# Splitting q and k once in the projection and storing them in three token orders, in a hybrid RWKV-7 and dilated-attention layer

## The chip, the cores and the metric

The kernel runs on one core of a Trainium2 chip, in one launch. The metric is device time in microseconds, the median of three runs. Engines are named as in the profile: PE (matmuls; PEld are its weight loads), DVE, ACT, POOL, and SP, whose queue starts most of the DMAs.

## The reference

One decoder layer over 2048 tokens of width 1024: a projection, two mixers side by side (an RWKV-7 recurrence on 512 columns, dilated attention with 8 heads of 64 on the other 512), an output projection, and a SwiGLU feed-forward of width 2816. What the change touches is the attention's three branches, which see the same q, k and v in three token orders:

```python
DILATED_PAIRS = ((128, 1), (512, 4), (2048, 16))
...
def to_sub(t):
    t = t.reshape(B, H, L, dilation, Dh).transpose(0, 1, 3, 2, 4)
...
s = jnp.einsum('bhrnqe,bhrnke->bhrnqk', qb, kc) * (Dh ** -0.5)
...
pe = jnp.exp(s - m)
den = jnp.sum(pe, axis=-1, keepdims=True)
o = jnp.einsum('bhrnqk,bhrnke->bhrnqe', pe, vc) / den
```

With dilation r, a token t belongs to the subsequence t mod r, and a query block of 128 of that subsequence sees its own and the previous block. The three results are mixed by a softmax over their log-sums.

## The kernel before

**Products in parts.** A float32 operand is written as a high part (rounded to the PE's fast format, `F32R`) plus a low part (the rest). A dense product is three matmuls of 128x512 (`three`, L220 to L223). Weights come through the class `Weights`: a DMA on SP's queue (L197), a cast on ACT for the high part (L207), a subtraction on DVE for the low part (L209), with 2 raw and 3 split buffers.

**Projection (0 to about 900 us).** `dense_in` takes four blocks of 512 tokens. For each it runs 26 column tiles `ct` of 128 columns; tiles 14 to 17 are q and 18 to 21 are k, two heads in each. Such a tile is copied from PSUM by ACT (L489) and written to the DRAM tensors `qT` or `kT` by one DMA on ACT's queue (L493). The RWKV recurrence runs beside it: a generator `drive` takes dense steps between its steps, and this fixes PE's order by hand. The other engines' orders are made by the scheduler. Tiles of the pool `sp` are shared by tag ("kx", "kkh", "Pd", "mshift" belong to the recurrence and to the token shift).

**Attention.** `heads_b` runs five parts: `attention(0)` (branches 1 and 2 of block 0, and block 0 of branch 3), `branch3` (all of dilation 16), `attention(1)`, `(2)` and `(3)`. Each goes over 8 heads and cuts a head into `Unit`s, 32 in each part. A unit computes scores on PE (L950, L951: q's high half against k's high and low part), mask and row minimum on DVE (L955), exponentials on ACT (L960), transposes on PE (L967) with a copy on ACT or DVE by turns (L971), and values (L981). Dense products of the output projection, and later of the feed-forward, are put between, again by `drive`, with a fixed cost `ATT` for each attention step.

Before a head's units its q and k are loaded and split. `load_dup` (L928 to L930) loads 64 rows twice, into both halves of the 128 partitions, from SP's queue. `split_q` (L921, L922) and `split_k` (L925, L926) then cast on ACT and subtract on DVE, once for the plain token order and once more through a strided view for dilation 4; `branch3` does the same with stride 16, four pieces of 512 tokens for q and for k of each head:

```python
q2 = qq[:, TB:].rearrange("p (r i) -> p r i", r=4)
...
split_q(q2, rq.rearrange("p (i r) -> p r i", r=4))
split_k(kh2, kl2, rk_all[:, TB - back :].rearrange("p (n i r) -> p r n i", r=4, i=P))
```

The split of head h+1 (`prep`) runs beside head h where a second set of buffers is free (`spare`, `q2nd`), else between the heads.

Of the kernel before, what the change touches and what calls it, by code (L numbers as in the profile page):

```python
# [37 lines left out]
BR = ((128, 1), (512, 4), (2048, 16))  # L38
NEG = -1.0e30
# [7 lines left out]
def tile_hybrid_layer(  # L47
# [41 lines left out]
    qT = dram.tile([W, S], F32, name="qT")  # L89
    kT = dram.tile([W, S], F32, name="kT")  # L90
# [140 lines left out]
    F_COST = 3.0, 1.0, 1.0, 0.0, 0.0  # L231
# [40 lines left out]
    def constants():  # L272
# [6 lines left out]
        for hi, low, src, tag, lo, zero in (  # L279
            (w2d, w2lo, decay_w2[0], "L", slice(0, HD), slice(HD, P)),  # L280
            (a2d, a2lo, iclr_a2[0], "kkh", slice(HD, P), slice(0, HD)),
        ):
            nc.gpsimd.memset(f32(low[zero]), 0.0)
            raw = sp.tile([P, W], F32, name="wa_raw", tag=tag)
# [84 lines left out]
    def dense_in():  # L369
# [58 lines left out]
        for b in range(nblocks):  # L428
            t0 = b * TB
            for at, ct in enumerate(ORDER):  # L430
# [26 lines left out]
                if ct < SHIFT_TILES:  # L457
# [28 lines left out]
                    got[b, ct] = o  # L486
                else:
                    o = sp.tile([P, TB], F32, name="qkv", bufs=1)
                    nc.scalar.copy(out=o, in_=pd)  # L489
                    if ct < 22:  # L490
                        dst = qT if ct < 18 else kT
                        r0 = ((ct - 14) % 4) * P
                        nc.scalar.dma_start(out=dst[r0 : r0 + P, t0 : t0 + TB], in_=o)  # L493
                    else:

                        def turn_v(o=o, ct=ct, t0=t0):
                            pt = ps_t.tile([P, NT, P], F32, name="pv", tag="t")
                            for i in range(NT):
                                nc.tensor.transpose(pt[:, i, :], o[:, i * P : (i + 1) * P], ident)
                            o2 = sp.tile([P, NT, 2, HD + 1], F32, name="vn", tag="mshift", bufs=1)  # L500
                            nc.gpsimd.memset(o2[:, :, :, HD : HD + 1], 1.0)
                            nc.scalar.copy(out=o2[:, :, :, 0:HD], in_=pt.rearrange("p i (h d) -> p i h d", d=HD))
                            h0 = (ct - 22) * 2
                            nc.scalar.dma_start(
                                out=vN[t0 : t0 + TB, h0 : h0 + 2, :].rearrange("(i p) h d -> p i (h d)", p=P),
                                in_=o2.rearrange("p i h d -> p i (h d)"),
                            )

                        later.append(turn_v)
                done.add((b, ct))  # L510

    def rwkv():
# [3 lines left out]
        for b in range(nblocks):  # L516
# [8 lines left out]
            def start_pair(j):  # L525
# [33 lines left out]
                Pd = sp.tile([P, NCH, CH + 1], F32, name="Pd")  # L559
# [40 lines left out]
            for j in range(NPAIR):  # L600
# [8 lines left out]
                kkh = sp.tile([P, TB], F32, name="kkh")  # L609
# [293 lines left out]
    R3 = BR[2][1]  # L903
# [15 lines left out]
    def split_q(hi, raw):  # L919

        nc.scalar.copy(out=hi, in_=raw)  # L921
        nc.vector.tensor_tensor(out=hi[HD:P], in0=raw[HD:P], in1=f32(hi[HD:P]), op=ALU.subtract)  # L922

    def split_k(hi, lo, raw):
        nc.scalar.copy(out=hi, in_=raw)  # L925
        nc.vector.tensor_tensor(out=lo, in0=raw, in1=f32(hi), op=ALU.subtract)  # L926

    def load_dup(dst, src):  # L928
        nc.sync.dma_start(out=dst[0:HD], in_=src)
        nc.sync.dma_start(out=dst[HD:P], in_=src)  # L930
# [5 lines left out]
    class Unit:  # L936
# [7 lines left out]
        def scores(self):  # L944
# [4 lines left out]
            for g, (q, kh, kl) in enumerate(self.group):  # L949
                nc.tensor.matmul(ps[:, g, :], lhsT=q, rhs=kh, start=True, stop=False)  # L950
                nc.tensor.matmul(ps[:, g, :], lhsT=q, rhs=kl, start=False, stop=True)  # L951
# [97 lines left out]
    NK = R3 * P  # L1049
    q_all = ap.tile([P, NK], F32R, name="q_all")  # L1050
    k_all = ap.tile([P, 2, NK], F32R, name="k_all")
    rk_all = ap.tile([P, 2 * TB], F32, name="rk_all")
    sides, spare = [], []

    def heads_of(head, prep, second, after):


        for h in range(HEADS):
            nxt = None
            if h + 1 < HEADS:  # L1060
                second[h + 1] = h % 2 == 0 and bool(spare)
                nxt = prep(h + 1)
            elif after:
                nxt = after()
                next(nxt)
            beside = second[h] or h + 1 < HEADS and second[h + 1]
            if nxt and beside:
                sides.insert(0, nxt)
            yield from head(h)
            if nxt and beside:  # L1070
                if nxt in sides:
                    sides.remove(nxt)
                for _ in nxt:
                    pass
            elif nxt:
                yield lambda nxt=nxt: nxt

    def attention(b):
# [4 lines left out]
        n1, n2 = TB + lead, TB + back  # L1083
        vs, raws, cur, second = {}, {}, {}, {0: False}
# [8 lines left out]
        def load_v(hp):  # L1093
# [10 lines left out]
            vs[hp] = v1, v2  # L1104

        def load_qk(h):
            hs = slice(h * HD, (h + 1) * HD)
            rq = ap.tile([P, TB], F32, name="rq", tag="rq", bufs=2)
            load_dup(rq, qT[hs, t0 : t0 + TB])
            load_dup(rk_all[:, TB - back :], kT[hs, t0 - back : t0 + TB])  # L1110
            raws[h] = rq

        def prep(h):
            rq = raws.pop(h)
            if second[h]:
                kh, kl = spare[0][:, 0, 0 : n1 + n2], spare[0][:, 1, 0 : n1 + n2]
            else:
                kh, kl = k_all[:, 0, 0 : n1 + n2], k_all[:, 1, 0 : n1 + n2]
            if second[h] and not b:

                qq = spare[0].rearrange("p a n -> p (a n)")[:, n1 + n2 : n1 + n2 + 2 * TB]
            else:
                qq = q_all[:, (h % 2) * 2 * TB : (h % 2 + 1) * 2 * TB]

            q1, kh1, kl1 = qq[:, 0:TB], kh[:, 0:n1], kl[:, 0:n1]
            split_q(q1, rq)
            split_k(kh1, kl1, rk_all[:, TB - lead :])
            yield 0.0

            q2 = qq[:, TB:].rearrange("p (r i) -> p r i", r=4)  # L1130
            kh2 = kh[:, n1:].rearrange("p (r n i) -> p r n i", r=4, n=nb)
            kl2 = kl[:, n1:].rearrange("p (r n i) -> p r n i", r=4, n=nb)
            split_q(q2, rq.rearrange("p (i r) -> p r i", r=4))
            split_k(kh2, kl2, rk_all[:, TB - back :].rearrange("p (n i r) -> p r n i", r=4, i=P))
            cur[h] = q1, kh1, kl1, q2, kh2, kl2
            if h + 1 < HEADS:
                load_qk(h + 1)
            yield 0.0
            yield False
            if h % 2 and h + 1 < HEADS:  # L1140
                load_v((h + 1) // 2)
            yield False

        def head(h):
            q1, kh1, kl1, q2, kh2, kl2 = cur.pop(h)
            v1, v2 = vs[h // 2]
            hl = h % 2
            for m0, m1 in ((0, 1), (1, 3), (3, 4)) if b == 0 else ((0, 2), (2, 4)):
# [542 lines left out]
```

## Time and profile before

| | us |
|---|---|
| runs, median (lowest to highest) | 3007.9 (3002.45 to 3013.22) |
| the profiled execution | 3003.22 |
| its span, first to last instruction | 3001.3 |
| PE busy | 2881.1 (96%) |
| PE weight loads busy | 2381.6 (79%) |
| DVE busy | 1957.3 (65%) |
| ACT busy | 1405.2 (47%) |
| POOL busy | 383.7 (13%) |
| bytes moved | 358.67 MB, mean 120 GB/s |

Busy is the time in which an engine executes; shares are of the whole span and hide that the stages differ. The granted clock is PE's speed as the throttle let it run, 1.00 being 2.4 GHz and 0.50 the lower level of 1.2 GHz. "Landing" is the time from a DMA's start on its queue to the arrival of its last byte.

### The profile page before, as it was taken

How to read it: one execution, taken by the hardware profiler on the slowest of the kernel's cores; microseconds unless marked ns; L12 is line 12 of the kernel's file. 1: busy time of each engine (PE TensorE's matmuls, PEld its weight loads, DVE VectorE, ACT ScalarE, POOL GpSimd, SP SyncE). 2: the span in 40 equal slices, each digit the busy share in tenths (PEclk: the TensorE clock that was granted, in tenths of full speed). 3: DMA queues.
4: the chain of work that ended last, by engine and by line, in shares of the span. 5: the costliest groups of instructions: out<-in, count | busy, mean ns of one | idle time of the engine just before them, and what ended most of it. 6: DMA issues, size and time to landing. Idle time of an engine off the chain costs nothing. (4 is left out here: it accounts for less than half of the span.)

```text
span 3001.3 us, 47441 instructions
## 1 busy us (share of the span) xinstructions
PE 2881.1 (96%) x17457; PEld 2381.6 (79%) x17457; DVE 1957.3 (65%) x3974; ACT 1405.2 (47%) x2688; POOL 383.7 (13%) x543
## 2 busy tenths in 40 slices
PE   8999999998998888899999999999999999999998
PEld 6777777776777777788888888888888888888887
DVE  6877788786868877766665585656675444554444
ACT  5534544544536666655544464434453332342233
POOL 1123113112103221000100010001010100000001
PEclk9999999999998999899999999999999999999999
DMA  4332332332233777454444454444344333333333
GB/s 127 102 100 74 94 104 78 100 105 60 61 100 117 226 230 240 133 140 124 128 146 118 132 157 119 117 125 124 113 138 127 107 101 97 102 120 98 96 98 102
DMA packets 456716, 358.67 MB, mean 120 GB/s; under 512 B 26610, under 2 KB 384548, under 8 KB 456484
## 3 DMA queue, kind: packets, MB, share of 16 engines
q1 hardware_dynamic: 419348, 318.35, 36.6%
q10 hardware_dynamic: 32656, 22.62, 2.5%
q0 software_dynamic: 4480, 14.68, 1.3%
q8 instruction: 137, 2.24, 0.3%
q14 instruction: 95, 0.78, 0.1%
HBM read 311.19 MB, written 44.37 MB: 118 GB/s over the span
## 5 line engine op out<-in xcount | busy, mean ns | idle before, releaser
L209 DVE TENSOR_TENSOR wlo<-wraw,whi 128x512 fp32r<-128x512 f32 x800 | 566.0, 708 | 618.4 <-ACT whi L207 613.3
L207 ACT CAST whi<-wraw 128x512 fp32r<-128x512 f32 x800 | 495.4, 620 | 944.3 <-PE acc L223 257.1
L221 PE MATMUL pd<-h_hi,whi 128*128 128x512 f32 (+1 forms) x840 | 350.6, 417 | 3.4 <-DVE r L466 1.6
L222 PE MATMUL pd<-h_lo,whi 128*128 128x512 f32 (+1 forms) x840 | 329.9, 393 | 1.0 <-DVE h_lo L386 0.8
L223 PE MATMUL pd<-h_hi,wlo 128*128 128x512 f32 (+1 forms) x840 | 329.7, 392 | 0.1
L221 PE MATMUL acc<-whi,a_hi 128*128 128x512 f32 x704 | 286.6, 407 | 0.7 <-DVE x L1505 0.7
L221 PE MATMUL pg<-fh_hi,whi 128*128 128x512 f32 x704 | 284.0, 403 | 1.9 <-ACT whi L207 1.3
L221 PE MATMUL pu<-fh_hi,whi 128*128 128x512 f32 x704 | 284.6, 404 | 0.0
L223 PE MATMUL acc<-whi,a_lo 128*128 128x512 f32 x704 | 276.0, 392 | 0.0
L223 PE MATMUL pu<-fh_hi,wlo 128*128 128x512 f32 x704 | 275.8, 392 | 0.0
L223 PE MATMUL pg<-fh_hi,wlo 128*128 128x512 f32 x704 | 275.8, 392 | 0.0
L222 PE MATMUL pg<-fh_lo,whi 128*128 128x512 f32 x704 | 274.6, 390 | 0.0
L222 PE MATMUL acc<-wlo,a_hi 128*128 128x512 f32 x704 | 274.5, 390 | 0.0
L222 PE MATMUL pu<-fh_lo,whi 128*128 128x512 f32 x704 | 274.4, 390 | 0.0
L960 ACT ACTIVATE pr<-pr,mx 128x256 f32<-128x256 f32 (+1 forms) x416 | 162.7, 450 | 104.9 <-DVE mx L955 104.6
L221 PEld LDWEIGHTS pd<-h_hi,whi 128*128 128x128 f32 x840 | 159.4, 190 | 38.8 <-issue 2.0
L223 PEld LDWEIGHTS pd<-h_hi,wlo 128*128 128x128 f32 x840 | 159.0, 189 | 35.9 <-DVE wlo L209 0.5
L222 PEld LDWEIGHTS pd<-h_lo,whi 128*128 128x128 f32 x840 | 159.8, 190 | 28.6 <-DVE h_lo L386 2.6
L987 POOL COPY oo<-mx 128x2 f32<-128x2 f32 (+2 forms) x160 | 50.8, 323 | 993.2 <-DVE mx L955 886.4
L981 PEld LDWEIGHTS po<-vv,pts 128*128 128x128 f32 x1008 | 151.6, 195 | 21.7 <-ACT oo L986 2.5
L223 PEld LDWEIGHTS pg<-fh_hi,wlo 128*128 128x128 f32 x704 | 132.1, 188 | 29.3 <-DVE wlo L209 0.4
L223 PEld LDWEIGHTS pu<-fh_hi,wlo 128*128 128x128 f32 x704 | 132.1, 188 | 29.2 <-DVE wlo L209 0.3
(581 smaller groups left out, 5536.9 us busy)
## 6 DMA issues: line engine op xcount, KB each, us to landing
wraw<-in_w_in_dram SPq DMA_DIRECT2D x208, 256.0 KB, 3.0
wraw<-in_w_gate_dram SPq DMA_DIRECT2D x176, 256.0 KB, 3.0
wraw<-in_w_up_dram SPq DMA_DIRECT2D x176, 256.0 KB, 2.9
wraw<-in_w_down_dram SPq DMA_DIRECT2D x176, 256.0 KB, 2.7
rq<-qT SPq DMA_DIRECT2D x128, 128.0 KB, 3.1
wraw<-in_w_out_dram SPq DMA_DIRECT2D x64, 256.0 KB, 4.4
rk_all<-kT SPq DMA_DIRECT2D x48, 256.0 KB, 4.3
rk_all<-kT SPq DMA_DIRECT2D x80, 128.0 KB, 3.7
```

Source lines behind the costliest of these rows:

```text
L207: nc.scalar.copy(out=hi, in_=raw)
L209: nc.vector.tensor_tensor(out=lo, in0=raw, in1=f32(hi), op=ALU.subtract)
L221: nc.tensor.matmul(ps, lhsT=lhs[0], rhs=rhs[0], start=first, stop=False)
L222: nc.tensor.matmul(ps, lhsT=lhs[0], rhs=rhs[1], start=False, stop=False)
L223: nc.tensor.matmul(ps, lhsT=lhs[1], rhs=rhs[0], start=False, stop=last)
L960: nc.scalar.activation(out=pr[:, g, :], in_=pr[:, g, :], func=AF.Exp, scale=-1.0, bias=mx[:, g])
L981: nc.tensor.matmul(po[:, g, :], lhsT=pts[:, g, kb, :], rhs=vb[g][kb], start=(kb == 0), stop=(kb == kbs - 1))
L987: nc.gpsimd.tensor_copy(out=o[:, :, OA:OW], in_=self.mxs[j])
```

## The change

In the projection a q or k tile is now split once: ACT casts the high part (`qk_hi`), DVE subtracts the low part (`qk_lo`) straight from PSUM. Each part is stored three times, in the plain order, in the order of dilation 4 and in that of dilation 16, in the DRAM tensors `qS` and `kS`. ACT makes the two reordered copies of the high part and starts its three DMAs; POOL makes those of the low part and SP starts them. The attention splits nothing any more: each unit loads its own q (two DMAs of 64 rows: high and low half) and k (four: two parts, each into both halves of the partitions), three units ahead. The buffers for raw q and k, and the second sets, are gone. PE's matmuls are the same 14651 rows in number and shapes; the k operand of branches 2 and 3 is read through a strided view.

```diff
+                elif ct < 22:
+                    hi = sp.tile([P, TB], F32R, name="qk_hi", tag="qkv", bufs=1)
+                    lo = sp.tile([P, TB], F32R, name="qk_lo", tag="kx", bufs=2)
+                    nc.scalar.copy(out=hi, in_=pd)
+                    nc.vector.tensor_tensor(out=lo, in0=pd, in1=f32(hi), op=ALU.subtract)
+                    rows_ = slice(((ct - 14) % 4) * P, ((ct - 14) % 4 + 1) * P)
+                    dst = qS if ct < 18 else kS
+                    for n, (part, copy, queue, tags) in enumerate((
+                        (hi, nc.scalar.copy, nc.scalar, (("mshift", 1), ("kkh", 1))),
+                        (lo, nc.gpsimd.tensor_copy, nc.sync, (("kx", 2), ("Pd", 1))),
+                    )):
+                        queue.dma_start(out=dst[0][n, rows_, t0 : t0 + TB], in_=f32(part))
+                        for d, r, (tag, bufs) in zip(dst[1:], (4, R3), tags):
+                            perm = sp.tile([P, r, TB // r], F32, name=f"qk{r}", tag=tag, bufs=bufs)
+                            copy(out=perm, in_=f32(part).rearrange("p (i r) -> p r i", r=r))
+                            if ct < 18 and r == R3:
+                                to = d[n, rows_].rearrange("p (r b i) -> p b r i", r=r, b=NB)[:, b]
+                                queue.dma_start(out=to, in_=perm)
...
-                    if ct < 22:
-                        dst = qT if ct < 18 else kT
-                        r0 = ((ct - 14) % 4) * P
-                        nc.scalar.dma_start(out=dst[r0 : r0 + P, t0 : t0 + TB], in_=o)
...
+    def load_q(src, h, c0, c1):
+
+        t = ap.tile([P, TB], F32R, name="q", tag="q", bufs=5)
+        for n in range(2):
+            nc.sync.dma_start(out=f32(t[n * HD : (n + 1) * HD, 0 : c1 - c0]), in_=src[n, h * HD : (h + 1) * HD, c0:c1])
+        return t
+
+    def load_k(h, src, parts):
+
+
+        t = ap.tile([P, 2, TB], F32R, name="k", tag="k", bufs=5)
+        for n in range(2):
+            view = parts(src[n, h * HD : (h + 1) * HD])
...
+            for e in range(2):
+                dst = t[e * HD : (e + 1) * HD, n, 0:size]
...
+                nc.sync.dma_start(out=f32(dst), in_=view)
...
+    def next_unit():
+        fetch(to_load, loaded)
+        return loaded.pop(0)
...
+        def load1(h, m0, m1):
+
+            c0 = t0 + (m0 - (b > 0 or m0 > 0)) * P
+            return load_q(qS[0], h, t0 + m0 * P, t0 + m1 * P), load_k(h, kS[0], lambda s: s[:, c0 : t0 + m1 * P])
...
-            split_q(q1, rq)
-            split_k(kh1, kl1, rk_all[:, TB - lead :])
...
-                split_k(kk[:, 0, :, ns], kk[:, 1, :, ns], ks.pop(0).rearrange("p (i r) -> p r i", r=R3))
...
-                split_q(q3[:, :, b * n : (b + 1) * n], qs.pop(0).rearrange("p (i r) -> p r i", r=R3))
...
+        for _ in range(3):
+            fetch(to_load, loaded)
+        yield 3.0
```

SP's queue where `attention(0)` begins, as the program before has it: behind 71 weight loads of the projection in a row, the four 64-row loads of head 0, two loads of v, and the loads of the next heads.

```order
L197 DMA wraw<-in_w_in_dram 128x4x128 x71
L929 DMA rq<-qT 64x512
L930 DMA rq<-qT 64x512
L929 DMA rk_all<-kT 64x512
L930 DMA rk_all<-kT 64x512
L1097 DMA vv<-vN 128x4x130
L1103 DMA vv<-vN 128x4x130
```

The same place after the change: first the last low part of the projection, then the loads of v and of head 0's four units.

```order
L507 DMA k_63<-qk_10202 128x512
L507 DMA k_64<-qk_10205 128x512
L1115 DMA vv<-vN 128x4x130
L1121 DMA vv<-vN 128x4x130
L940 DMA q<-q_59 64x128 x2
L954 DMA k<-k_62 64x128 x4
L940 DMA q<-q_59 64x256 x2
L954 DMA k<-k_62 64x384 x4
L940 DMA q<-q_59 64x128 x2
L954 DMA k<-k_62 64x256 x4
L940 DMA q<-q_60 64x512 x2
L954 DMA k<-k_63 64x512 x4
```

A head of block 0 takes 24 such loads where it took 4. From the first q load to the first of `branch3` the queue now holds 192 loads of q and k, 33 others and 11 of weights; through `branch3` 192, 38 and 41.

SP's queue in the projection, block 0, tiles 14 to 17, after the change (before, this stretch holds weight loads alone):

```order
L499 DMA q_59<-qk_lo 128x512
L507 DMA q_60<-qk_1672 128x512
L505 DMA q_61<-qk_1675 2048x1x32
L499 DMA q_59<-qk_lo 128x512
L507 DMA q_60<-qk_1745 128x512
L505 DMA q_61<-qk_1748 2048x1x32
L199 DMA wraw<-in_w_in_dram 128x4x128 x2
L499 DMA q_59<-qk_lo 128x512
L507 DMA q_60<-qk_1822 128x512
L505 DMA q_61<-qk_1825 2048x1x32
L199 DMA wraw<-in_w_in_dram 128x4x128 x2
```

The weight loads, which nothing separated, now stand behind DMAs that wait for DVE (`qk_lo`) and for POOL's reordered copies; the dilation-16 order of q is written in runs of 32 numbers (128 bytes).

ACT's order at the first q tile, before:

```order
L489 COPY qkv<-pd 128x512 [waits PE_49]
L493 DMA qT<-qkv 128x512 [waits Activation_49]
L207 CAST whi<-wraw 128x512 [waits DMAHW6_49,DVE_49,PE_49]
```

and after:

```order
L491 CAST qk_hi<-pd 128x512 [waits PE_49]
L499 DMA q_59<-qk_hi 128x512 [waits Activation_49]
L502 COPY qk_1665<-qk_hi 128x512 [waits DMAHW5_49]
L502 COPY qk_1668<-qk_hi 128x512
L507 DMA q_60<-qk_1665 128x512 [waits Activation_49]
L505 DMA q_61<-qk_1668 2048x1x32 [waits Activation_49]
L209 CAST whi<-wraw 128x512 [waits DMAHW6_49,DVE_49,PE_49]
```

Two copies and two DMAs come between a tile's cast and the next weight cast. The waits named DMAHW0 to DMAHW7 are eight counters that the DMAs of SP and ACT take in turn, so a DMA can have to wait for one that is eight places earlier.

## Rows read from the trace of the kernel before

**Rows 1.** Busy time by stage (stretch, length, engines, PE clock, DMA share, GB/s)
```profile
core 0: us, PE busy (x) PEld busy (x) DVE busy (x) ACT busy (x) POOL busy (x), PEclk, DMA share, GB/s
150.00:225.00 75.00, 71.20 (x816) 56.09 (x816) 54.89 (x107) 29.89 (x63) 15.05 (x18) 0.98 0.35 100
...
825.00:900.00 75.00, 72.82 (x673) 57.58 (x671) 49.43 (x106) 26.89 (x52) 5.84 (x10) 1.00 0.33 100
...
909.70:1072.10 162.40, 138.91 (x1122) 119.92 (x1123) 138.80 (x388) 111.31 (x255) 46.88 (x74) 0.87 0.59 179
1072.10:1319.50 247.40, 215.06 (x1212) 183.95 (x1211) 176.70 (x457) 159.17 (x313) 31.59 (x63) 0.92 0.66 188
1319.50:2336.50 1017.00, 1011.93 (x5214) 851.88 (x5213) 638.17 (x1257) 489.85 (x892) 102.21 (x153) 1.00 0.44 128
```

**Rows 2.** Timeline of PE: first score matmuls of attention(0), branch3, attention(1)
```profile
909.68 0.47 PE L950 MATMUL s_att<-k_all,q_all 128*128 128x128 f32 x1 [4.69 <-ACT k_all L925]
...
1072.12 0.22 PE L950 MATMUL s_att<-k_all,q_all 128*128 128x128 f32 x1
...
1319.47 0.28 PE L950 MATMUL s_att<-k_all,q_all 128*128 128x256 f32 x1
```

**Rows 3.** What PE waited for, 898.8 to 1319.5 us (total, times, longest)
```profile
PE pt_att L967 <- DVE pts L971: 14.4, 6, 5.9
PE pt_att L967 <- ACT pts L971: 6.9, 6, 3.0
```

**Rows 4.** Splits by form on DVE, then on ACT, 898.8 to 1319.5 us (busy us, mean ns | idle)
```profile
L922 DVE TENSOR_TENSOR q_all<-rq,q_all 64x512 fp32r<-64x512 f32 x32 | 31.1, 978 | 7.2 <-ACT q_all L921 6.6
L926 DVE TENSOR_TENSOR k_all<-rk_all,k_all 128x512 fp32r<-128x512 f32 x28 | 27.4, 987 | 7.2 <-ACT k_all L925 7.1
L926 DVE TENSOR_TENSOR k2nd<-rk_all,k2nd 128x512 fp32r<-128x512 f32 x20 | 20.2, 1021 | 1.4 <-ACT k2nd L925 1.2
...
L922 DVE TENSOR_TENSOR q2nd<-rq,q2nd 64x512 fp32r<-64x512 f32 x12 | 12.5, 1044 | 6.7 <-ACT q2nd L921 6.5
...
L921 ACT CAST q2nd<-rq 128x512 fp32r<-128x512 f32 x12 | 13.0, 1089 | 5.0 <-DMA rq<-qT 5.0
```

**Rows 5.** Timeline of SP's queue: 64-row loads one behind the other
```profile
899.98 0.60 SPq L929 DMA_DIRECT2D rk_all<-kT  x1
900.62 0.60 SPq L930 DMA_DIRECT2D rk_all<-kT  x1
```

**Rows 6.** What SP's queue waited for, 898.8 to 1319.5 us
```profile
SPq L1596 <- DMA x1p<-xh: 21.2, 12, 5.9
...
SPq L1301 <- DMA o2D<-oo: 8.0, 2, 6.8
...
SPq L1304 <- DMA o3A<-o3a: 6.6, 2, 3.7
...
SPq L1425 <- DMA x<-in_x_dram: 4.4, 3, 1.9
```

**Rows 7.** DMA queue of SP over the span; then issues (KB each, median us to landing)
```profile
q1 hardware_dynamic: 419348, 318.35, 36.6%
...
rq<-qT SPq DMA_DIRECT2D x128, 128.0 KB, 3.1
wraw<-in_w_out_dram SPq DMA_DIRECT2D x64, 256.0 KB, 4.4
...
xh<-in_x_dram SPq DMA_DIRECT2D x24, 256.0 KB, 5.3
```

**Rows 8.** Prices for the projection's new work: ACT's DMA issue, a POOL pass, a DVE pass
```profile
L493 ACTq DMA_DIRECT2D qT<-qkv x16: 326/332/339, 160.0 to 868.0; - x16
...
L586 POOL TENSOR_TENSOR W<-r,Pd 128x512 f32<-128x512 f32 x12 | 15.2, 1270 | 0.0
...
L386 DVE TENSOR_TENSOR h_lo<-pt,h_hi 128x512 fp32r<-128x512 f32 x32 | 22.0, 687 | 4.0 <-ACT h_hi L385 4.0
```

**Rows 9.** ACT's weight casts, 1319.5 to 2336.5 us, and what ended their idle time
```profile
L207 ACT CAST whi<-wraw 128x512 fp32r<-128x512 f32 x300 | 185.5, 618 | 313.3 <-PE acc L223 106.0 <-PE pu L222 54.2 <-PE pg L222 42.1
```

More of the change, by code (lines that the diff above doesn't have):

```diff
@@ L38 @@
 BR = ((128, 1), (512, 4), (2048, 16))
+R3 = BR[2][1]
 NEG = -1.0e30
@@ L283, in constants @@
             nc.gpsimd.memset(f32(low[zero]), 0.0)
-            raw = sp.tile([P, W], F32, name="wa_raw", tag=tag)
+            raw = sp.tile([P, W], F32, name="wa_raw", tag=tag, bufs=1)
             for h in range(2):
@@ L1048, in tile_hybrid_layer, with heads_of @@
     oo2 = ap.tile([P, NT, HEADS, OW], F32, name="oo2")
[L1049 to L1055, printed above, removed]
-        for h in range(HEADS):
[L1059 to L1068, printed above, removed]
-            yield from head(h)
[L1070 to L1076, printed above, removed]
+    sides = []
+    def heads_of(head):
+        for h in range(HEADS):
+            if h % 2:
+                fetch(v_load, v_loaded)
+            yield from head(h)
     def attention(b):
@@ L1082, in attention @@
         nb = 2 if b else 1
-        n1, n2 = TB + lead, TB + back
-        vs, raws, cur, second = {}, {}, {}, {0: False}
+        vs = {}
         def out1():
@@ L1144, in head @@
+        for h in range(HEADS):
+            if h % 2 == 0:
+                v_load.append(lambda hp=h // 2: load_v(hp))
+            for m in blocks:
+                to_load.append(lambda h=h, m=m: load1(h, *m))
+            for r in groups:
+                to_load.append(lambda h=h, r=r: load2(h, *r))
         def head(h):
-            q1, kh1, kl1, q2, kh2, kl2 = cur.pop(h)
-            v1, v2 = vs[h // 2]
+            if h % 2 == 0:
+                vs[0] = v_loaded.pop(0)
+            v1, v2 = vs[0]
@@ L1147, in head @@
             hl = h % 2
-            for m0, m1 in ((0, 1), (1, 3), (3, 4)) if b == 0 else ((0, 2), (2, 4)):
+            for m0, m1 in blocks:
+                q, k = next_unit()
                 two = b > 0 or m0 > 0
@@ L1176, in head @@
                 yield Unit(
-                    [(q2[:, r, :], kh2[:, r, 0, :], kl2[:, r, 0, :]) for r in range(4)], P,
+                    [[t[:, r * P : (r + 1) * P] for t in (q, *k)] for r in range(4)], P,
                     [(amask[:, P:], vb, oo2[:, :, h, :]), (mask4, vb, o3)], keep,
@@ L1188, in head @@
                     )
-        def first():
-            load_qk(0)
-            load_v(0)
-            yield 0.0
-            yield from prep(0)
-        return first, lambda after: heads_of(head, prep, second, after)
+        return lambda: heads_of(head)
     def branch3():
-        qs, ks, v3s, cur, second, q2nd = [], [], {}, {}, {0: False}, {}
-        qtodo = [(h, b) for h in range(HEADS) for b in range(NB)]
-        ktodo = list(qtodo)
-        n = TB // R3
+        vs = {}
         o3 = oo2.rearrange("p a h w -> p (a h w)").rearrange("p (r h w) -> p r h w", r=R3, h=2)
-        def load_q():
-            if qtodo:
-                h, b = qtodo.pop(0)
-                rq = ap.tile([P, TB], F32, name="rq3", tag="rq", bufs=2)
-                load_dup(rq, qT[h * HD : (h + 1) * HD, b * TB : (b + 1) * TB])
-                qs.append(rq)
@@ L1247, in head @@
+            return v3
+        for h in range(HEADS):
+            if h % 2 == 0:
+                v_load.append(lambda hp=h // 2: load_v3(hp))
+            for r0 in range(0, R3, 4):
+                to_load.append(lambda h=h, r0=r0: load3(h, r0))
         def head(h):
-            q3, kh3, kl3 = cur.pop(h)
             hl = h % 2
-            if hl and h + 1 < HEADS:
-                load_v3((h + 1) // 2)
-            v3 = v3s[h // 2]
+            if not hl:
+                vs[0] = v_loaded.pop(0)
+            v3 = vs[0]
@@ L1266, in head @@
                 )
-        def first():
-            q2nd[0] = fp.tile([P, NK], F32R, name="q1st", tag="gb", bufs=1)
-            for _ in range(2):
-                load_q()
-                load_k()
-            load_v3(0)
-            yield 0.0
-            yield from prep(0)
-        return first, lambda after: heads_of(head, prep, second, after)
+        return lambda: heads_of(head)
     def heads_b():
@@ L1281, in heads_b @@
         parts = attention(0), branch3(), attention(1), attention(2), attention(3)
-        for _, cost in zip(parts[0][0](), F_COST):
-            yield cost
-        for n, (_, units) in enumerate(parts):
-            yield from units(parts[n + 1][0] if n + 1 < len(parts) else None)
+        fetch(v_load, v_loaded)
+        for _ in range(3):
+            fetch(to_load, loaded)
+        yield 3.0
+        for n, units in enumerate(parts):
+            yield from units()
             if n == 0:
```

154 lines of the change are left out of this document (57 added, 97 removed).

## The prediction

> **What bounds the kernel now.** The first view to read is the table of busy times by stage, because the shares over the whole span hide that there are two kinds of stage. From 1319.5 us to 2336.5 us PE is busy 1011.93 of 1017.0 us at full clock [rows 1]: there nothing that another engine is spared can be worth anything. The projection is almost as full (71.20 of 75 us and 72.82 of 75 us in two stretches where q and k tiles are made). Between them lie two stages, bounded by the first score matmuls of `attention(0)`, `branch3` and `attention(1)` [rows 2], that are not full:
>
> - A, `attention(0)`, 162.4 us: PE busy 138.91, granted clock 0.87, DVE busy 138.80 (85%).
> - B, `branch3`, 247.4 us: PE busy 215.06, clock 0.92, DVE busy 176.70, ACT 159.17.
>
> A clock of 0.87 between the levels 1.00 and 0.50 means 26% of A, 42 us, at 1.2 GHz; the same work at full clock would have taken half of that, so 21 us. With the idle time, 23.5 us, A holds 44 us that PE could get back, and its floor is 118 us. In the same way B holds 32.3 us of idle and 16% (39.6 us) at the lower level, worth 20: 52 us, floor 195. In these stages the clock is low where PE has stood idle, so both parts go together.
>
> What PE waits for comes next: transposed scores whose one PSUM buffer is not yet copied out by DVE (14.4 us) or ACT (6.9 us) [rows 3]. These copies are short; they are late because they queue behind the splits. The splits shown on DVE are 31.1 + 27.4 + 20.2 + 12.5 = 91 us of the 315 us that DVE is busy in A and B, each about 1 us long, with a cast of the same length on ACT ahead of it [rows 4]. So A and B are bounded by DVE and ACT, and all that the change can win lies there: at most 44 + 52 = 96 us.
>
> **The sum, part by part**, against the profiled execution's own 3003.2 us (the median of the runs, 3007.9, lies 4.7 above it).
>
> *Taken out of A and B:* the splits. DVE falls to about 100 us in A (32 splits of its 8 heads, and the first head of `branch3`, near 39 us) and to about 115 in B, well under PE's floors. DVE ceases to bound. What is late next is the loading.
>
> *Put into A:* 192 loads of 64 rows on SP's queue, six to a unit, where there were some 32. One behind the other such loads start 0.64 us apart [rows 5]. So 192 x 0.64 = 123 us, and the 44 other DMAs of that stretch at about 0.45 us (an estimate between the 0.33 us of a 128-row issue [rows 8] and the 0.60 of [rows 5]) make 20 more: 143 us. They begin later than now: the queue first issues the last low part of k, which waits for DVE (0.69) and two POOL copies (1.27 each), so near 903 us instead of 898.8. The queue is free at 1046 at the earliest. It also blocks, in order, on writes that have to land first: 8.0 + 6.6 + 4.4 = 19 us in this stretch [rows 6], if they stay. With 3 us to land, A ends between 1049 and 1068; I take 1058, **14 us earlier** than the 1072.1 of now. A rule of the Trainium skill speaks against just this form of loading: "DMA: Bandwidth & Descriptors", section "Rules for kernel authors", says that two transfers to disjoint partition halves serialize and should be one of 128 partitions. The trace agrees in so far as two 64-row starts one behind the other take 1.28 us [rows 5]; the number that counts is already in the sum.
>
> *Put into B:* SP issues 192 x 0.64 + 79 x 0.45 = 159 us, plus 21 us of blocking on `x1p` [rows 6]: 180. The DMA engines: a unit of `branch3` now loads 768 KB where a piece of 512 KB did, so 8.4 MB more in 32 units; SP's queue moved 318.35 MB in 36.6% of the span, 290 GB/s at full share [rows 7], so 29 us more on top of 0.66 x 247.4 = 163: 192 us. PE's floor is 195. Three resources within 15 us of each other don't overlap perfectly, and a DMA share near 0.9 has no row here (the highest stage has 0.66), so I take 215 between the bounds of 195 and 247: **32 us saved**.
>
> *Put into the projection, 32 tiles:* on ACT 64 strided copies at 1.09 us (the strided cast of [rows 4]) and 64 more DMA starts at 0.33 us: 91 us. On DVE 32 subtractions from PSUM at 0.69 us: 22 us. On POOL 64 copies: no such row, so its 1270 ns pass over 128x512 [rows 8], 81 us. For one stretch of 8 tiles this raises ACT from 29.89 to about 53 of 75 us, DVE from 54.89 to 60, POOL from 15.05 to 35 [rows 1]. All of it is covered by idle time on those engines while PE runs dense products; if the cover fails, it is because the recurrence's short copies on ACT and updates on DVE come behind a 1.1 us copy. Weight loads on SP now stand behind DMAs that wait for POOL's copies, about 4 us after a tile's end, but each is needed only after two buffers of raw and three of split weights are used up. Bounds: zero (nothing is removed here that PE waits for, which excludes a gain) and 57 us (DVE's 22 plus one exposed ACT copy for each tile, 35). Most is covered, so **10 us lost**.
>
> *After 1319.5 us:* the splits that go were free there. The 576 loads that come cost SP 369 of 1017 us, and a weight load can stand behind six of them, 3.8 us. ACT's casts of weights wait mostly for PE to free a buffer, not for DMA (106 + 54 + 42 of 313 us of their idle time) [rows 9], so weights are early by some microseconds. Bounds 0 and 30; **5 us lost**.
>
> Sum: -14 - 32 + 10 + 5 = -31 us, so 2972 for an execution like the profiled one, and 4.7 more, **2977 us**, for the median.
>
> **Rivals.**
>
> *Loads limited by eight in flight, slower.* The queue's DMAs take eight counters in turn, so one starts only when that eight places back has landed. At 0.64 us apart this does not bind while a load lands within 8 x 0.64 = 5.1 us; now the q loads land in 3.1, but weights of the output projection in 4.4 and x in 5.3 [rows 7], and the DMA share goes from 0.66 to about 0.9. At 7 us a start costs 0.875: A takes 236 x 0.875 = 206 us from 903 and ends 41 us later than now (with the 3 to land), B needs 271 x 0.875 = 237, 10 saved; with the projection's 10 and 10 later it is 51 us slower, 3054, or 3059 for the median. The point from which it decides is a landing of 6.2 us (0.775 a start: A +18, B -32, +15). For it speaks the spread of [rows 7]; against it that q's own loads are short. Chance 0.22.
>
> *Starting a DMA costs little, much faster.* Then A and B are bounded by PE and the DMA engines alone: A by 0.59 x 162.4 + 10.5 MB / 290 GB/s = 96 + 36 = 132 us, 30 saved; B near 200, 47 saved; with 7 lost elsewhere, 70 us faster, 2938 for the median. The same page of the Trainium skill, section "Issuing engines are not separate DMA queues", holds that the time to start a DMA is usually small beside the DMA. The trace bears it out weakly: 0.60 us a start against 3.1 us to land, but starts add up on one queue and landings overlap. Chance 0.12.
>
> *Nothing that can be told.* The queue's blocking waits all stay, so A ends where it does now; B saves 25, and the projection costs 25 because ACT's longer queue delays the recurrence. The sum is zero: 3008. Chance 0.14.
>
> That the splits stay after all is excluded: the program's order has none left in the attention.
>
> **How the numbers follow.** My forecast has 0.52, the rivals 0.22, 0.12 and 0.14. A measurement of this kernel tells about 0.3%, 9 us, from no change. Faster than that: the second rival and the forecast but for the edge of its own range, 0.61. Slower: the first rival and the case that the projection costs its upper bound, 0.26. Same: 0.13. The forecast's own range, from the bounds of A (1049 to 1072), B (195 to 235) and the two losses, is 2940 to 3010; to hold 8 in 10 it must reach into the first rival, so 2938 to 3048.
>
> **What would show it.** If the steps are right, the profile after shows DVE and ACT well below PE in A and B, A ending near 1058 and B lasting some 215 us, SP's queue starting loads back to back through A, and PE waiting in score matmuls for q and k by DMA instead of in transposes. ACT's busy time falls little (about 204 us of casts go, 70 come), DVE's by some 180. Wrong would be: score matmuls of A that never wait for a load (then starts are cheap), starts more than 0.78 us apart (then eight in flight decide), or a projection that ends after about 925 us.

## The result: 3.4% slower, and the profile after

The changed kernel takes 3112.7 us (median of 4 runs, 3101.85 to 3116.85) against 3009.85 of the kernel before in the same job; the ratio is 1.034 with a 95% interval of 1.0305 to 1.0374. The forecast was 2977, in a range of 2938 to 3048. The profiled execution has a span of 3107.7 us, 106.4 more than before. Both traces hold 17457 matmuls of PE; the 14651 named ahead stand in no view of them.

The busy times by stage (stretch, length, engines with busy us, PE clock, DMA share, GB/s) answer to [rows 1]: two stretches in which q and k tiles are made, then `attention(0)`, `branch3` and the three parts behind them, each bounded by its first score matmul as in [rows 2].

```profile
150.00:225.00 75.00, 64.86 (x679) 50.01 (x677) 55.59 (x98) 39.63 (x65) 26.38 (x26) 0.93 0.81 197
900.00:950.00 50.00, 39.97 (x384) 29.74 (x383) 39.72 (x65) 23.42 (x30) 16.96 (x14) 0.90 1.03 228
979.05:1167.87 188.82, 140.32 (x1126) 119.79 (x1127) 104.49 (x344) 79.25 (x213) 40.70 (x73) 0.82 0.68 185
1167.87:1422.47 254.60, 218.69 (x1208) 186.94 (x1207) 112.44 (x391) 99.95 (x247) 26.25 (x61) 0.91 0.89 235
1422.47:2439.13 1016.66, 1012.29 (x5214) 851.84 (x5213) 542.12 (x1177) 406.77 (x811) 86.04 (x154) 1.00 0.58 165
```

- Up to the first score matmul: 909.7 us before, 979.0 now, **69.3 more**.
- A, `attention(0)`: 162.4 us before, 188.8 now, **26.4 more**, although DVE is busy 104 us in place of 139 and ACT 79 in place of 111.
- B, `branch3`: 247.4 before, 254.6 now, **7.2 more**, with DVE at 112 in place of 177.
- `attention(1)` to `attention(3)`: 1016.7 in place of 1017.0. What follows: 668.6 in place of 664.8.

So the splits did leave A and B, and the time did not. Two thirds of the loss lie in the projection. Set side by side matmul by matmul, PE's rows of the two traces show where: the delay is 0 until the first q tile (150 us), stands at 15 from 260 to 380 us, at 32 from 480 to 600, at 48 from 740 to 840, and at 66 by 900. It grows in the four stretches that make q and k tiles, with a tile or two behind them, and hardly anywhere else. What PE waits for up to 980 us (total, times, longest), and in the second piece what ACT's weight cast waits for:

```profile
PE pd L225 <- DVE wlo L211: 22.7, 12, 4.7
PE xp L831 <- DVE suv L886: 17.4, 12, 3.3
...
PE pd L223 <- ACT whi L209: 5.1, 4, 2.1
```
```profile
ACT whi L209 <- DMA wraw<-in_w_in_dram: 70.2, 32, 6.0
```

Before, PE never waited for a split weight in these tiles; now it waits 27.8 us for them. The granted clock in the first of the two stretches above is 0.93 where it was 0.98 [rows 1], so products are slower too after such a wait. SP's queue in the second block (start, length, line, instruction):

```profile
407.92 0.34 SPq L499 DMA_DIRECT2D q<-qk_lo  x1
409.18 0.34 SPq L507 DMA_DIRECT2D q<-qk  x1
410.37 0.53 SPq L505 DMA_DIRECT2D q<-qk  x1
414.29 0.39 SPq L199 DMA_DIRECT2D wraw<-in_w_in_dram  x1
```

The weight load of 414.29 stands behind three stores. It is cast at 418.76, as soon as it has landed; over the pieces loaded between 640 and 700 us a cast begins on average 5.6 us after the load's start (13 pieces), where it was 11.3 before (9), when the weights lay ready for some microseconds. Three things could be the reason: the place behind the stores, the 128-byte runs of q's last order, or the copies; a fourth is the sheer bytes.

In A, PE waits for keys and for weights where it waited for copies of transposed scores [rows 3]:

```profile
PE s_att L989 <- DMA k<-k: 21.1, 8, 8.3
PE acc L223 <- ACT whi L209: 16.1, 3, 6.5
```

And SP's queue there, where nothing holds it up, starts loads 0.64 us apart (2.51 us for four in a row):

```profile
1054.11 2.51 SPq L954 DMA_DIRECT2D k<-k  x4
1056.72 1.36 SPq L940 DMA_DIRECT2D q<-q  x2
1058.13 2.52 SPq L954 DMA_DIRECT2D k<-k  x4
1060.69 0.58 SPq L199 DMA_DIRECT2D wraw<-in_w_out_dram  x1
```

### The profile page after: what moved, and what is told of

The parts are those of the page before. It is cut to its first block, busy times and chain, and to the rows that moved or that the text cites. A ratio compares the mean times of both kernels' runs of the same rounds, so it can differ in the third digit from the quotient of the medians.

```text
span 3107.7 us, 48620 instructions
## 1 busy us (share of the span) xinstructions
PE 2914.0 (94%) x17457; PEld 2399.7 (77%) x17457; DVE 1802.6 (58%) x3814; ACT 1295.2 (42%) x2560; POOL 432.5 (14%) x607
## 5 line engine op out<-in xcount | busy, mean ns | idle before, releaser
L223 PE MATMUL pd<-h_hi,whi 128*128 128x512 f32 (+1 forms) x840 | 357.2, 425 | 8.8 <-ACT whi L209 5.1
L225 PE MATMUL pd<-h_hi,wlo 128*128 128x512 f32 (+1 forms) x840 | 337.1, 401 | 22.7 <-DVE wlo L211 22.7
L994 DVE CUSTOM_DVE_ANT_0 pr<-s_att,amask 128x256 f32<-128x256 f32 (+1 forms) x384 | 122.8, 362 | 113.1 <-PE s_att L990 112.7
L1026 POOL COPY oo<-mx 128x2 f32<-128x2 f32 (+2 forms) x160 | 36.8, 234 | 1026.5 <-DVE mx L994 910.7
```

The lines of the kernel that those rows point to most:

```text
L223: nc.tensor.matmul(ps, lhsT=lhs[0], rhs=rhs[0], start=first, stop=False)
L225: nc.tensor.matmul(ps, lhsT=lhs[1], rhs=rhs[0], start=False, stop=last)
L994: nc.vector.tensor_tensor_reduce(out=pr[:, g, :], in0=ps[:, g, :], in1=mask, scale=-0.125, scalar=-NEG, op0=ALU.add, op1=ALU.min, accum_ou ...
L1026: nc.gpsimd.tensor_copy(out=o[:, :, OA:OW], in_=self.mxs[j])
```

## The experiments

Start is that of the first score matmul, "1 to 3" the length of `attention(1)` to `attention(3)`; all from the traces, in us. Ratios are to the kernel before, with their 95% interval.

| kernel | start | A | B | 1 to 3 | median | ratio |
|---|---|---|---|---|---|---|
| before | 909.7 | 162.4 | 247.4 | 1017.0 | | 1 |
| changed | 979.0 | 188.8 | 254.6 | 1016.7 | 3112.7 | 1.034 (1.0305 to 1.0374) |
| e1 low parts by POOL's queue | 974.2 | 195.4 | 249.7 | 1018.7 | 3100.6 | 1.032 (1.0292 to 1.0348) |
| e2 q in blocks | 973.1 | 192.4 | 264.3 | 1014.0 | 3113.7 | 1.0364 (1.034 to 1.0387) |
| e3 no copies | 968.3 | 194.0 | 249.3 | 1013.4 | 3101.1 | 1.0322 (1.0292 to 1.0352) |
| e4 three DMAs per unit | 961.5 | 164.9 | 235.9 | 1012.8 | 3048.7 | 1.0154 (1.0125 to 1.0182) |
| e5 e1 to e3 together | 962.4 | 192.9 | 247.6 | 1014.4 | 3097.3 | 1.0318 (1.0297 to 1.0338) |
| e6 one order stored | 911.3 | 191.8 | 254.1 | 1014.7 | 3043.8 | 1.0129 (1.0112 to 1.0146) |
| e7 k by the block | 967.4 | 156.2 | 228.4 | 1034.1 | 3055.3 | 1.0164 (1.0146 to 1.0181) |
| e8 natural order | 917.5 | 156.6 | 235.4 | 1034.2 | 3007.6 | 1.0009 (0.9998 to 1.0021) |
| e9 the same, k copied | 913.6 | 159.1 | 231.0 | 1013.4 | 2985.6 | 0.9932 (0.9913 to 0.9951) |
| e10 two orders stored | 927.0 | 197.2 | 257.2 | 1014.6 | 3064.2 | 1.0196 (1.0172 to 1.022) |
| e11 before, no subtractions | 910.5 | 150.6 | 238.3 | 1014.2 | 2981.3 | 0.994 (0.992 to 0.9961) |

### What costs the projection 69 us: e1, e2, e3

```diff
-                        (lo, nc.gpsimd.tensor_copy, nc.sync, (("kx", 2), ("Pd", 1))),
+                        (lo, nc.gpsimd.tensor_copy, nc.gpsimd, (("kx", 2), ("Pd", 1))),
```


> The three stores of each low part start from POOL's own queue instead of SP's; nothing else changes. Three theories for the 69 us by which attention(0) begins later than before (979.0 against 909.7 us). Queue order: weight loads on SP stand behind stores that wait for POOL's copies; then attention(0) begins near 945 here and the time falls by 30 to 40 us against the changed kernel (3112.7). Descriptors: the q stores of dilation 16, in runs of 128 bytes, fill the DMA engines; then it stays within 10 us of 979. Copies: the two copies on ACT and the two on POOL for each tile, and the tiles that they share with the recurrence, hold things up; then within 10 us of 979 too, or later, since POOL also has to start the stores.

```diff
+    out=perm.rearrange("p (g i c) -> p g i c", g=4, c=4),
+    in_=f32(part).rearrange("p (i g c) -> p g i c", g=4, c=4),
...
-    [[q[:, r * P : (r + 1) * P]] + [t[:, r] for t in ks] for r in range(4)], P,
+    [[q.rearrange("p (i c) -> p c i", c=4)[:, r]] + [t[:, r] for t in ks] for r in range(4)], P,
```


> The dilation-16 order of q is stored block by block in rows of 2 KB (128 descriptors in place of 2048), with four residues interleaved, and loaded as four runs of 512 bytes per row as k's is; the number of loads, stores and copies stays. Descriptors: DMA share in the q tiles' stretches falls from 0.84 to 1.03 to about 0.5, weights land in 4 us again, and attention(0) begins near 940, 40 us earlier than in the changed kernel. Queue order or copies: it begins within 10 us of 979. In branch3 the q loads have four runs per row in place of one, which should cost at most 5 us there.

```diff
-                            perm = sp.tile([P, r, TB // r], F32, name=f"qk{r}", tag=tag, bufs=bufs)
-                            copy(out=perm, in_=f32(part).rearrange("p (i r) -> p r i", r=r))
+                            perm = f32(part).rearrange("p (r i) -> p r i", r=r)
```


> Leaves out the permuting copies of q and k on ACT and POOL (the dilated orders are stored straight from the parts, so the attention of dilation 4 and 16 gets q and k in a wrong order); all stores and loads stay in number and size. Copies: attention(0) begins near 940. Queue order: it gains too, some 30 us, since SP's stores wait for POOL no more. Descriptors: it stays within 10 us of 979, as the 128-byte stores are all there.

Measured: `attention(0)` begins at 974.2, 973.1 and 968.3. **None of the three alone is the cause**; each gives back 5 to 11 of 69 us. In e1 no weight load stands behind such a store on SP, and PE waits for split weights as long as in the changed kernel (27.3 us for `wlo`). In e3 PE waits for `wlo` only 1.4 us, but ACT now waits 51.9 us for stores that still read the one buffer of the high part, which the copies had let go sooner.

e2 showed something else. Its score matmuls of B read the stationary operand (the one that PE loads before a matmul, here q) with a step of 16 bytes; the moving operand (k) streams past it. Groups of PE in B (busy us, mean ns | idle), in the changed kernel and then in e2:

```profile
L989 PEld LDWEIGHTS s_att<-k,q 128*128 128x128 f32 x120 | 24.2, 201 | 2.7 <-DVE fh_lo L1386 1.8
...
L989 PE MATMUL s_att<-k,q 128*128 128x128 f32 x120 | 29.0, 278 | 1.2 <-DVE fh_lo L1386 1.2
```
```profile
L999 PEld LDWEIGHTS s_att<-k,q 128*128 128x128 f32 x116 | 37.7, 325 | 2.2 <-DVE fh_lo L1396 1.2
...
L999 PE MATMUL s_att<-k,q 128*128 128x128 f32 x116 | 43.4, 374 | 0.8 <-DVE fh_lo L1396 0.8
```

A weight load takes 325 ns instead of 201, and B is 9.7 us longer than in the changed kernel: that gave back what e2 won earlier.

### Whether it is the bytes: e5, e6, e10

e5 makes the three edits together:

> All three of the single edits together on the changed kernel: no permuting copies, low parts stored from POOL's queue, every store in rows of 2 KB (so the dilated orders hold wrong orders of q and k). The six stores of 256 KB per q or k tile stay. Theory that queue order, 128-byte runs and copies each cost a part and one takes over when another goes: attention(0) begins near 915 to 930, and the time falls by 45 to 60 us against the changed kernel's 3112.7. Theory that what is written (1.5 MB per tile in place of 0.25, against the weights' 0.5 MB) is too much for the DMA engines beside the weights: attention(0) begins after 950, though DMA starts wait for nothing else.

e6 drops the two dilated orders:

```diff
-    qS, kS = ([dram.tile([2, W, S], F32, name=f"{t}{r}") for r in (1, 4, 16)] for t in "qk")
+    qS, kS = ([dram.tile([2, W, S], F32, name=t)] * 3 for t in "qk")
...
-                        for d, r, (tag, bufs) in zip(dst[1:], (4, R3), tags):
+                        for d, r, (tag, bufs) in ():
```


> Leaves out the two dilated orders altogether: no copies and two stores per tile (high and low part), and all loads read the one natural order (so dilation 4 and 16 get wrong orders); the loads stay in number and nearly in size. By both theories of the run before, the projection's loss goes: attention(0) begins between 910 and 925. If it begins after 940, the cost lies in the subtraction on DVE and the second store, that is in splitting in the projection at all. attention(0) and branch3 should last as in the changed kernel (189 and 255 us), since SP's starts are the same.

e10 is e5 with one of the two dropped:

```diff
-                        for d, r, (tag, bufs) in zip(dst[1:], (4, R3), tags):
+                        for d, r in ((dst[2], R3),):
```


> As the run with all three edits (no copies, low parts stored from POOL's queue, rows of 2 KB), but the dilation-4 order isn't stored either (its loads read the natural order, so dilation 4 and 16 get wrong orders): four stores of 256 KB per tile. Before the last tiles of the projection the delay against the kernel before was 2.5 us with two stores and 52.2 with six. If the delay goes with the bytes it is near 25 us here; if it is a matter of the DMA engines being full (share 0.85 to 0.93 with six stores, 0.31 to 0.47 with two), four stores still fit (share near 0.65) and it is under 12 us.

The same 50 us of the third block in e5 (six stores per tile), e10 (four) and e6 (two); the last two columns are the DMA share and GB/s. By then the three are at different tiles; over the four whole stretches of q and k tiles the shares are 0.79 to 0.94, 0.55 to 0.78 and 0.35 to 0.47.

```profile
640.00:690.00 50.00, 42.41 (x466) 31.83 (x464) 33.35 (x64) 15.91 (x31) 15.12 (x23) 0.86 0.88 212
```
```profile
640.00:690.00 50.00, 43.46 (x608) 32.73 (x601) 36.01 (x66) 21.66 (x46) 19.00 (x25) 0.93 0.55 151
```
```profile
640.00:690.00 50.00, 47.18 (x632) 36.39 (x630) 40.48 (x73) 21.95 (x49) 14.08 (x16) 0.97 0.31 95
```

With six stores, no copies, no short runs and no store on SP, `attention(0)` still begins at 962.4. With two it begins at 911.3. By 900 us of the kernel before, PE is 2.5, 20.0 and 52.2 us late with two, four and six stores, and 65.7 in the changed kernel. So **the two dilated orders are the cost**: without them 63 of the 66 us are gone. They raise what is written per tile from 0.5 MB (0.25 before the change) to 1.5. And the more is written, the later weights land. Where ACT's weight cast has to wait for its load, in the q and k tiles and the two tiles behind them, the load took 3.6 us from its start to the cast before (mean of 13), 3.2 in e6 (10), 5.2 in e10 (23), 6.4 in e5 (20) and 5.4 in the changed kernel (24); in the other tiles 3.0 to 3.4 in all of these.

How the 66 us divide among bytes, number of stores and copies isn't shown. The number of stores falls together with the bytes. And e5 loses its time in another place than the changed kernel. What PE and ACT wait for in e5 up to 950 us:

```profile
PE pd L223 <- DVE qk_lo L492: 11.1, 5, 4.7
```
```profile
ACT qk_hi L491 <- DMA q<-qk_hi: 30.2, 8, 5.8
```

PE waits for a split weight only 0.6 us there, where the changed kernel has 27.8; it waits for the subtraction that frees its PSUM tile, and that is late because, without copies, three stores read the one buffer of the high part. So the 13 us between 52 and 66 are not the worth of the other causes, and e7 below speaks against bytes alone.

e10's two expectations were 25 (it goes with the bytes) and under 12 (only full engines cost); 20 is nearer to the first. e6 also shows that the split itself, a cast, a subtraction and a second store, is nearly free, and that A's loss (191.8 us) has nothing to do with the projection.

### What costs A and B: e4 and e7

```diff
-                        queue.dma_start(out=dst[0][n, rows_, t0 : t0 + TB], in_=f32(part))
+                        queue.dma_start(out=dst[0][rows_, n, t0 : t0 + TB], in_=f32(part))
...
-        for n in range(2):
-            nc.sync.dma_start(out=f32(t[n * HD : (n + 1) * HD, 0 : c1 - c0]), in_=src[n, h * HD : (h + 1) * HD, c0:c1])
+        view = src[h * HD : (h + 1) * HD].rearrange("p n c -> (p n) c")
+        nc.sync.dma_start(out=f32(t[:, 0 : c1 - c0]), in_=view[:, c0:c1])
...
+        dst = t[:, 0 : m * y].rearrange("(p e) (m y) -> e p m y", e=2, m=m)
+        for e in range(2):
+            nc.sync.dma_start(out=f32(dst[e]), in_=view)
```


> q and k are kept with the high and low part of a row next to each other, so that a unit is loaded by three DMAs (q one of 128 rows, k two of 64 rows with twice the bytes per row) instead of six of 64 rows; the bytes stay. Theory that SP's starts bound attention(0) (150.6 us of starts in 189 us): the starts of a unit fall from 3.84 to about 1.65 us, attention(0) falls from 188.8 to 140 to 155 us and branch3 from 254.6 to 220 to 235, together 55 to 80 us less. Rival, that the DMA engines bound (share 0.68 and 0.89): attention(0) stays over 175 and branch3 over 248, under 20 us less. The start of attention(0) stays at 979 by both.

```profile
961.50:1126.30 164.80, 136.87 (x1126) 120.25 (x1127) 103.83 (x344) 78.91 (x213) 39.00 (x73) 0.83 0.74 212
1126.30:1362.30 236.00, 212.12 (x1209) 180.73 (x1208) 115.11 (x397) 102.52 (x253) 27.61 (x64) 0.94 0.88 262
```

Half the starts, the same bytes: A falls by 24 us and B by 19, 43 together, under the 55 to 80 expected but far over the rival's 20. SP's starts take 78 of A's 165 us where they took 151 of 189. **The number of DMA starts on one queue bounded A**; B is bounded by them in part. The Trainium skill, "DMA: Bandwidth & Descriptors", section "Rules for kernel authors", asks for one transfer of 128 partitions in place of two to disjoint halves; e4 agrees with the advice.

The start, which was expected to stay at 979, came 17.5 us earlier. The stores of the projection are the same in number and bytes, but with the high and low part of a row side by side in DRAM PE is 50.6 us late by 900 us and not 65.7, and the weight loads that ACT waits for take 4.3 us (mean of 19) and not 5.4. Why the new layout costs less is not shown.

e7 goes on with a load per head and block, and no dilation-4 order of k:

> On the kernel with three DMAs per unit: k is stored in natural and in dilation-16 order only, dilation 4 reads the natural order with a step of four elements as the moving operand, and a head's k and q are loaded once per block (4 DMAs per head and block in place of 12, in branch3 8 per head). Four stores per k tile in place of six. If the moving operand's step costs PE nothing: attention(0) begins near 950, lasts 140 to 155 us, branch3 215 to 235, and attention(1) to attention(3) together stay at 1013 us, so 2985 to 3020 in all. If a step of 16 bytes slows it as it slowed the stationary operand in the run with q in blocks (275 to 397 ns for 128 columns), the 512 products of dilation 4 cost some 60 us more, mostly in attention(1) to attention(3), and the time is over 3040.

A falls to 156.2 and B to 228.4, but parts 1 to 3 are 21 us longer than in e4. The start is not earlier either: with 1.25 MB written per tile in place of 1.5, PE is 53.9 us late by 900 us, e4 50.6, and in both it waits some 27 us for split weights. e10, with 1 MB, no copies and no short runs, is 20.0 late at nearly the same DMA share (0.55 to 0.78; e7 has 0.56 to 0.75). So bytes are not the whole of it, and what the copies and short runs add to them stays open. The 350 ns in e8's expectation (e7's mean over both dilations) understate the step's price; e8 has it by itself.

### A version from these findings: e8 and e9

```diff
-                    for n, (part, copy, queue, tags) in enumerate((
...
+                    for n, (part, queue) in enumerate(((hi, nc.scalar), (lo, nc.sync))):
+                        queue.dma_start(out=dst[rows_, n, t0 : t0 + TB], in_=f32(part))
...
+            k2 = [k[:, n].rearrange("p (i r) -> p r i", r=4) for n in range(2)]
...
+                    perm_q(out=q2, in_=f32(q).rearrange("p (i r) -> p r i", r=4))
```


> Drawn from the runs before: q and k are split once in the projection and stored in natural order only (two stores per tile, high and low part of a row next to each other); attention loads a head's q and k once per block (three DMAs; in branch3 block by block, twelve per head) and makes the other orders on the chip: q by a copy on POOL, k by a step of 4 or 16 elements in the moving operand. Projection's loss near 3 us (attention(0) begins at 910 to 916), attention(0) 150 to 160 us, branch3 220 to 240 (the step of 16 has no row so far; if it costs no more than the step of 4, 283 to 350 ns for 256 columns, some 15 us), attention(1) to attention(3) some 20 us longer than in the changed kernel from the step of 4 (1017 + 20). Sum 2965 to 2995, faster than both kernels. Rival: POOL's copies, with the wait for their loads ahead of them in POOL's queue, hold up attention(0) and branch3; then these last as long as before (410 us together) and the time is over 3010.

e9 adds, in the last three parts:

```diff
+                    if b:
...
+                        for n in range(2):
...
+                            perm_k(out=kp[n], in_=f32(k2[n]))
```


> As the run with natural order, but in attention(1) to attention(3) k is put into dilation-4 order by two POOL copies per head, so that the moving operand is contiguous there. If the step of 4 is what costs 20 us there, attention(1) to attention(3) last 1013 to 1020 us again and the time is 15 to 20 us less than with the step. If POOL's copies (about 5 us per head) come too late for the head or slow DVE, it is the same or more.

e8 is as fast as the kernel before, not faster (3007.6). Its parts came out near what was expected of them, but those parts, with the 668 us behind `attention(3)`, add up to 2985 to 3021 and not to the 2965 to 2995 that were written down. Its score matmuls of dilation 4 and of dilation 1 in parts 1 to 3, both with 256 columns (busy us, mean ns | idle):

```profile
L967 PE MATMUL s_att<-kA,qp 128*128 128x256 f32 x64 | 26.7, 417 | 0.0
...
L967 PE MATMUL s_att<-kA,qn 128*128 128x256 f32 x64 | 16.6, 282 | 0.0
```

A step of 16 bytes in the moving operand costs 135 ns on 256 columns; 192 such matmuls there are 26 us, and parts 1 to 3 are 17 us longer than before. e9 removes it with POOL copies (PE busy 1012.05 of 1013.4 us), and is **faster than both kernels**, by 0.7% against the one before: 2985.6 us, 0.9932 (0.9913 to 0.9951).

```profile
913.60:1072.70 159.10, 140.07 (x1127) 123.58 (x1128) 108.18 (x344) 79.46 (x215) 55.33 (x89) 0.83 0.63 187
1072.70:1303.70 231.00, 207.21 (x1209) 179.81 (x1208) 116.34 (x398) 101.01 (x251) 68.83 (x123) 0.94 0.79 245
1303.70:2317.10 1013.40, 1012.05 (x5215) 851.75 (x5214) 573.79 (x1168) 405.08 (x804) 216.19 (x221) 1.00 0.46 140
```

### What the splits cost in the kernel before: e11

```diff
-        nc.vector.tensor_tensor(out=lo, in0=raw, in1=f32(hi), op=ALU.subtract)
...
-                nc.tensor.matmul(ps[:, g, :], lhsT=q, rhs=kl, start=False, stop=True)
+                nc.tensor.matmul(ps[:, g, :], lhsT=q, rhs=kh, start=False, stop=True)
```


> The kernel before without its 205 us of split subtractions on DVE (the scores take the high part of k in place of the low one, and q's low half is its rounded whole, so the scores differ a little); casts on ACT, loads, the projection and PE's order stay. By the prediction's reading, that attention(0) and branch3 are bounded by DVE and ACT and hold 44 and 52 us that PE could get back, these two fall from 410 us by 40 us or more together. Rival, drawn from the runs with few loads (attention(0) 156 to 165, branch3 228 to 236 us with no splits at all): their length is mostly the chain of short dependent steps of a unit with PE's clock low in between, and they fall by under 20 us. Where the projection ends and attention(1) to attention(3) stay as they are by both.

A falls by 11.8 us and B by 9.1, 20.9 together: just over the rival's 20, half of the 40 that the reading called for. ACT's casts are still there, so this is DVE's half of the splits alone. The waits for copies of transposed scores that the prediction had blamed on the splits hardly go (A and B, against [rows 3]):

```profile
PE pt_att L965 <- DVE pts L969: 9.5, 5, 6.1
PE pt_att L965 <- ACT pts L969: 8.1, 7, 3.2
```

## Why the prediction was wrong, step by step

- **The projection, +10 forecast, +69.3 measured: the step that failed most.** Its bounds were 0 and 57, so even they missed. What failed is the cover: the prediction held that weights stay ahead of PE, each "needed only after two buffers of raw and three of split weights are used up", and PE waited 27.8 us for split weights where it had waited for none. The prices of ACT's copies, DVE's subtraction and POOL's copies held:

```profile
L502 ACT COPY qk<-qk_hi 128x512 f32<-128x512 f32 x64 | 69.0, 1112 | 19.5 <-DMA q<-qk 8.9 <-ACT qk_hi L491 3.2 <-DMA k<-qk 3.2
...
L492 DVE TENSOR_TENSOR qk_lo<-pd,qk_hi 128x512 fp32r<-128x512 f32 x32 | 21.9, 685 | 10.0 <-ACT qk_hi L491 7.9 <-issue 1.1 <-DMA q<-qk_lo 0.9
...
L502 POOL COPY qk<-qk_lo 128x512 f32<-128x512 f32 x64 | 76.3, 1217 | 155.4 <-DVE qk_lo L492 110.1 <-DVE ss L360 31.6 <-DVE suv L886 4.7
```

  It had 1.09, 0.69 and 1.27 us for them. It counted bytes for B and none for the projection, where the dilated orders cost 63 of 66 us (e6). A sum of bytes alone would not have given it away: 8 tiles x 1.25 MB more are 10 MB, 34 us at the 290 GB/s of [rows 7], in 75 us that had a share of 0.35 [rows 1], so 0.81 of the engines, which is what the rows after show, and still under 1. What gives first is the time to land (3.6 us before, 5.4 now, above), with weights held two raw pieces deep; that tiles which wait to be written hold their buffers shows in e3 and e5.
- **A, 14 us earlier forecast, 26.4 longer measured.** The mechanism was named rightly ("SP's queue starting loads back to back", DVE no longer the bound, PE waiting for k by DMA), and e4 shows it. The starts were priced right: from the first q load to the first of `branch3` there are 236, and they take 141.9 us, forecast 143. What was mis-sized is beside them: the queue stands still between starts for 38.7 us, where 9 were taken of at most 19, and 16.3 us pass from `branch3`'s first load to its first score matmul, where 3 were put. And the loads begin at 970.9 us, because of the projection, not at 903.
- **B, 215 forecast, 254.6 measured.** The 271 starts from `branch3`'s first load on take 164.9 us, near the 159 forecast, but SP's queue stands still between them for 82.6 us and not for 21. No run got B under 228, far from "PE's floor is 195".
- **"A and B are bounded by DVE and ACT", 96 us to be won.** This reading failed in size. e11 takes DVE's half of the splits out and wins 21 us. e9, with no split in A and B and 87 starts in A, has A at 159 us, PE's clock at 0.83 and PE still idle for 19 us (159.1 less 140.07) where it was 23.5. The clock is low there with the splits gone as well, so "its floor is 118" was never in reach of this change.
- **Later parts, +5 forecast:** -0.3 in parts 1 to 3 and +3.8 behind them. The sum is right by luck: the loads that it priced cost nothing, and the 3.8 come where no q or k is loaded.
- **The rivals.** Slower was given 0.26, 0.22 of it for another reason and the rest for a projection at its upper bound. Starts are not over 0.78 us apart with eight in flight; only 8 of A's 202 q and k loads took over 1 us to start. That a start costs little is refuted by e4. The bound that the prediction set for itself, a projection that ends after 925 us, was crossed.

Open: what holds A at 150 to 165 us once neither SP nor the splits do; the 2 to 4 us behind `attention(3)` that all versions with loads of ready parts show; and how the projection's loss divides among bytes, stores and copies. Not tried: a third raw weight piece in the projection.

## What to carry to other kernels

When work moves from one stage to another, count its bytes on the DMA engines in the stage that takes it, and ask what there is loaded only a piece or two ahead; here its loads were late at a share of 0.55 to 0.78 (e10), with no engine full. Count DMA starts per queue as work of their own, and lay data out in DRAM so that one start fills 128 partitions. Store one order and make the others on an idle engine; a busy engine whose waits you can see is worth what an experiment without its work gives back, not the whole of its stage's idle time.

## What was not expected of the hardware

- A stationary operand read with a step of 16 bytes loads in 325 ns instead of 201 (means in B), and its matmul of 128 columns takes 374 to 399 ns instead of 278 to 285 (e2).
- A moving operand with a step of 16 bytes takes 417 ns instead of 282 for 256 columns; with a step of 64 bytes and 128 columns, in B, 300 to 308 against 278 to 285 (e8; transposes in the same stretches take 299 against 295, so the clock explains little of it).
- Loads land later well before the DMA engines are full: with four stores per tile (e10), at shares of 0.55 to 0.78 over the q and k tiles, the weight loads that ACT waited for took 5.2 us, with two stores (e6, 0.35 to 0.47) 3.2.
- The same bytes in the same number of stores cost less in another DRAM layout: shares of 0.61 to 0.81 over the q and k tiles in e4, 0.71 to 0.94 in the changed kernel, at about the same GB/s (177 to 226 and 175 to 208).
